# A planner's rule for work that two engines may do: GpSimd leaves it while VectorE has an earlier SBUF operation ready

## The chip, the core and the metric

The kernel runs on one core of a Trainium2 chip. The core has a matrix engine (TensorE, PE in the profile, with its weight loads as PEld), three elementwise engines (VectorE = DVE, ScalarE = ACT, GpSimd = POOL) and SyncE (SP), which here issues every DMA. Each engine runs its own list of instructions in order and waits on semaphores for the others. SBUF is the memory that all engines read; PSUM is where TensorE writes. The metric is the device time of one execution in microseconds, as the median of several runs.

## The reference

One inference step of a two-layer network on two groups of tokens with shared weights, 512 latent and 128 context tokens, 640 in all, width 1024:

```
for each of 2 layers:
  shift, scale, gate (twice) from SiLU(cond) @ ada_w + ada_b
  h = x * (1 + scale) + shift;  one projection h @ w_in, split among
    A  retention, both directions       B  gated linear attention, both directions
    C  differential attention (two softmax maps)      and three sigmoid merge gates
  merged = sum of sigmoid(m) * (y @ w_branch);  x = LayerNorm(ALPHA*x + gate * merged @ w_out)
  h = x * (1 + scale) + shift;  a, b = h @ ffn_w_up
  x = LayerNorm(ALPHA*x + gate * (gelu(conv3(a)) * b) @ ffn_w_down)
```

It returns both groups' outputs, and the context tokens' attention keys and values and final states.

## The kernel before

Activations stay in SBUF, features on the 128 partitions and the 640 tokens along a row: 8 rows of 128x640 are one activation. Weights are streamed in blocks of 128x1024 (`weights`, two blocks ahead of use, three buffers each for `w`, `whi` and `wlo`). Every product of float32 numbers is made of three fast ones: each operand is split into a rounded part and the rest (`whi` = rounded `w` on ScalarE, `wlo = w - whi`), and `gemm` adds hi\*hi, hi\*lo and lo\*hi. Tokens are handled in two halves, 384 and 256 wide, at the ends of a block of layers, so that a norm's first half runs beside the products of the second.

The kernel doesn't issue instructions directly. The text adds operations to a `Program` in the order in which the algorithm is written down; each has its possible engines, a cost per engine, its operands, and a key: its place in the text, plus `late` (the norm's operations have -300, so they count as 300 places earlier). `Program.order` calls `place`, a list scheduler: it keeps for every engine the time from which it is free and two heaps, `now` (operations ready by then, by key) and `later` (by the time from which they could start), picks a candidate for every engine, and places the candidate that starts first (a tie goes to the engine that stands first in PE, ACT, DVE, POOL, SP). The result, a list in order of planned start, is what the chip is given; the chip's engines then wait for what they need.

Most operations have one engine. Those marked `ANY` may go to VectorE or GpSimd, and these are the shared work of the title: `wlo` of every weight block, the rests `sal`, `vl`, `sql` of activations (`parts`), `ql` (`twice`), `kk` and `qd` (`stack`), and the chained sums of squares `sq` in `norm`. Planned costs in ns of n elements a row: 150 + 1.042 n on VectorE, 150 + 2.2 n on GpSimd. GpSimd also has work of its own: sums of gates `g`, rotary `sw`, decays `G`, `H`, `la`, and the rescaling of `xa`.

The plan has a `port`: a time before which no operation of that engine may start if its list `port` names the engine. An operation with SBUF operands alone names both ("DVE" and "POOL"); one that reads PSUM names only "POOL", so a VectorE operation that reads PSUM neither waits for the port nor takes it. Choosing for GpSimd, `place` looks first through `now`; a shared operation there is left waiting if VectorE would finish it no later. Candidates taken from `later` are not asked that. VectorE is asked before GpSimd, and its candidate has then been taken off `now["DVE"]`.

The norms, at four places, are these: a product with a matrix of 1/1024 gives the mean in PSUM (`pm`), VectorE subtracts it from eight rows `xa` (in the second half from a copy `mu` in SBUF), ScalarE squares, sums of squares give the variance, Ln and Exp on ScalarE give `rs`, and `hf`, `hh`, `hl` are the next products' operands. VectorE adds the products' results to `xa` before that (`xa<-pout` and `xa<-pdn`, the residual).

Of the kernel before, what the change touches and what calls it, by code (L numbers as in the profile page):

```python
# [223 lines left out]
class Program:  # L224
# [69 lines left out]
    def place(self, ahead, ahead_load, fences):  # L294
        import heapq
        engs = ("PE", "ACT", "DVE", "POOL", "SP")
        free = {e: 0.0 for e in engs}
        now, later = {e: [] for e in engs}, {e: [] for e in engs}
# [17 lines left out]
        def slots(op, t0):  # L316

            used = {}
            for t in op.tiles:
                if t.slot is None and t.pool is not None:  # L320
                    p = t.pool
                    u = used.get(p, 0)
                    used[p] = u + 1
                    if len(p.free) <= u + sum(n for (q, f), n in fences.items() if q is p and not f.eng and op.idx > f.idx):
                        p.blocked.append(op)
                        return None
                    if p.inorder or len(p.free) <= p.reserve:
                        while p.want[p.ptr][1].slot is not None:
                            p.ptr += 1
                        i, rank = p.ptr, 0  # L330
                        lim = 1 if p.inorder else len(p.free)
                        while rank < lim and p.want[i][1] is not t:
                            rank += p.want[i][1].slot is None
                            i += 1
                        if rank >= lim:
                            p.blocked.append(op)
                            return None
                    t0 = max(t0, heapq.nsmallest(u + 1, p.free)[u][0])
            return t0
# [4 lines left out]
        while len(done) < len(self.ops):  # L344
            best = None
            for e in engs:
                f, n, q = free[e], now[e], later[e]
                while q and (q[0][0] <= f or q[0][2].eng):
                    r, i, op = heapq.heappop(q)
                    if not op.eng:  # L350
                        heapq.heappush(n, (i, op))
                cand, skipped, waiting = None, [], []
                while n or q:
                    if n:
                        i, op = heapq.heappop(n)
                        if op.eng:
                            continue
                        t = slots(op, f)
                        if t is not None and e in op.port:
                            t = max(t, port)  # L360
                        if t is None:
                            op.queues.discard(e)
                            continue
                        if t > f:
                            heapq.heappush(q, (t, i, op))
                            continue
                        if e == "POOL" and len(op.engs) > 1 and max(free["DVE"], op.ready) + op.cost["DVE"] <= t + op.cost[e]:
                            waiting.append((i, op))
                            continue
                        if e == "ACT" and op.func in TABLES and not table & TABLES[op.func] and passed < 6 and len(skipped) < 6 \  # L370
                                and op.key[0] >= op.idx:
                            skipped.append((i, op))
                            continue
                        cand = (t, i, op)
                        break
                    if skipped:
                        break
                    r, i, op = heapq.heappop(q)
                    if op.eng:
                        continue  # L380
                    t = slots(op, r)
                    if t is not None and e in op.port:
                        t = max(t, port)
                    if t is None:
                        op.queues.discard(e)
                        continue
                    if t > r:
                        heapq.heappush(q, (t, i, op))
                        continue
                    cand = (t, i, op)  # L390
                    break
                if cand is None and skipped:
                    i, op = skipped.pop(0)
                    cand = (f, i, op)
                for x in skipped + waiting:
                    heapq.heappush(n, x)
                if cand is not None:
                    if best is None or cand[0] < best[0][0]:
                        if best is not None:
                            heapq.heappush(later[best[1]], best[0])  # L400
                        best = (cand, e)
                    else:
                        heapq.heappush(later[e], cand)
# [1351 lines left out]
```

## Time and profile before

| | |
|---|---|
| median of 3 runs | 2501.42 us (2501.3 to 2507.76) |
| the profiled execution | 2504.05 us, span 2502.3 us, granted clock 0.995 |
| TensorE busy | 2441.7 us (98% of the span) |
| VectorE, ScalarE, GpSimd busy | 1618.1, 1113.7, 528.8 us |
| wlo on VectorE | 268 instructions, 340.8 us, 1273 ns each |
| wlo on GpSimd | 50 instructions, 123.7 us, 2477 ns each |

The first part of the page gives busy time and its share of the span for each engine; a busy TensorE may still be slower than its best, since its products overlap. The line "A <- B: t, n, m" of the waits says that A waited for B for t us in total, n times, at most m. A line of the timeline gives start, duration, engine, source line and operation; "x2" means that two like instructions in a row were merged.

### The profile page before, as it was taken

What the parts mean: (1) busy time and instruction counts of PE and PEld (TensorE: products, weight loads), DVE (VectorE), ACT (ScalarE), POOL (GpSimd) and SP (SyncE); (2) the same over time, 40 slices, a digit from 0 to 9 for tenths busy, and PEclk for the clock granted to TensorE, in tenths of its full rate; (3) what the DMA queues carried; (4) which work ended last, traced back from release to release, by engine and by line L of the source; (5) the groups of instructions that cost most, each with busy time, mean ns of one, the idle gap of its engine ahead of it and who ended that gap; (6) DMA issues with size and microseconds to landing.
All of it is one profiled execution on the core that took longest, in us unless ns stands there. A gap on an engine that the chain in (4) does not pass through costs nothing.

```text
span 2502.3 us, 41620 instructions
## 1 busy us (share of the span) xinstructions
PE 2441.7 (98%) x16826; PEld 2328.8 (93%) x16826; DVE 1618.1 (65%) x2902; ACT 1113.7 (45%) x1815; POOL 528.8 (21%) x389
## 2 busy tenths in 40 slices
PE   8999999999999999999989999999999999999997
PEld 4898999999998999999978999999999999999997
DVE  4677778667798955656867677675454764343446
ACT  3576655444426322213456676554444353132234
POOL 0433112002153500000346521111013341000001
PEclk9999999999999999999999999999999999999999
DMA  7213222342543333333432133222314222222222
GB/s 291 79 60 123 100 87 89 113 161 86 185 136 103 126 109 118 104 125 124 137 101 84 64 127 101 87 95 70 107 67 144 94 84 76 76 73 71 77 77 87
DMA packets 99551, 263.85 MB, mean 105 GB/s; under 512 B 11168, under 2 KB 17696, under 8 KB 99232
## 3 DMA queue, kind: packets, MB, share of 16 engines
q1 hardware_dynamic: 99360, 261.21, 31.1%
q8 instruction: 132, 2.16, 0.4%
q14 instruction: 59, 0.48, 0.1%
HBM read 243.34 MB, written 17.83 MB: 104 GB/s over the span
## 4 chain that ended last, share of the span: by engine, by line
PE 90%; DVE 6%; ACT 2%; issue 1%; DMA 1%; SPq 0%; ACTq 0%; DVEq 0%
PE pmm L536 12%; PE pfb L536 12%; PE pfa L536 12%; PE pdn L536 12%; PE pvv L536 7%; PE pbr L536 6%; PE pout L536 4%; PE pcq L536 2%; PE pck L536 2%; PE pag L536 2%; PE psc L545 2%; PE pr L536 2%; PE ptc L536 1%; PE psl L545 1%; PE paq L536 1%
## 5 line engine op out<-in xcount | busy, mean ns | idle before, releaser
L557 ACT ACTIVATE whi<-w 128x1024 fp32r<-128x1024 f32 (+1 forms) x318 | 330.6, 1041 | 813.6 <-PE pdn L536 218.7
L569 DVE TENSOR_TENSOR wlo<-w,whi 128x1024 fp32r<-128x1024 f32 (+1 forms) x268 | 340.8, 1273 | 328.6 <-ACT whi L557 324.7
L569 POOL TENSOR_TENSOR wlo<-w,whi 128x1024 fp32r<-128x1024 f32 (+2 forms) x50 | 123.7, 2477 | 1190.9 <-ACT whi L557 991.5
L536 PE MATMUL pmm<-hh,whi 128*128 128x384 f32 (+1 forms) x768 | 240.9, 314 | 0.0
L536 PE MATMUL pmm<-hh,wlo 128*128 128x384 f32 (+1 forms) x768 | 240.7, 313 | 0.0
L536 PE MATMUL pmm<-hl,whi 128*128 128x384 f32 (+1 forms) x768 | 240.2, 313 | 0.0
L536 PE MATMUL pfa<-hh,whi 128*128 128x384 f32 (+1 forms) x704 | 218.1, 311 | 2.4 <-ACT hh L557 2.3
L536 PE MATMUL pfa<-hl,whi 128*128 128x384 f32 (+1 forms) x704 | 217.4, 310 | 2.6 <-DVE hl L583 2.6
L536 PE MATMUL pdn<-fl,whi 128*128 128x384 f32 (+1 forms) x704 | 218.5, 310 | 0.0
L536 PE MATMUL pdn<-fh,whi 128*128 128x384 f32 (+1 forms) x704 | 218.1, 310 | 0.0
L536 PE MATMUL pfb<-hh,whi 128*128 128x384 f32 (+1 forms) x704 | 217.9, 310 | 0.0
L536 PE MATMUL pfb<-hh,wlo 128*128 128x256 f32 (+1 forms) x704 | 217.4, 309 | 0.4 <-DVE wlo L569 0.4
L536 PE MATMUL pdn<-fh,wlo 128*128 128x384 f32 (+1 forms) x704 | 217.8, 309 | 0.0
L536 PE MATMUL pfa<-hh,wlo 128*128 128x384 f32 (+1 forms) x704 | 217.7, 309 | 0.0
L536 PE MATMUL pfb<-hl,whi 128*128 128x384 f32 (+1 forms) x704 | 217.4, 309 | 0.0
L536 PEld LDWEIGHTS pmm<-hh,whi 128*128 128x128 f32 x768 | 144.6, 188 | 3.1 <-issue 0.5
L536 PEld LDWEIGHTS pmm<-hh,wlo 128*128 128x128 f32 x768 | 144.6, 188 | 3.0 <-issue 1.1
L536 PEld LDWEIGHTS pmm<-hl,whi 128*128 128x128 f32 x768 | 144.5, 188 | 1.7 <-issue 0.5
L536 PE MATMUL pvv<-whi,hh 128*128 128x256 f32 (+1 forms) x480 | 137.4, 287 | 2.0 <-ACT whi L557 1.1
L536 PE MATMUL pvv<-wlo,hh 128*128 128x256 f32 (+1 forms) x480 | 136.0, 285 | 1.4 <-ACT z L557 0.7
L536 PE MATMUL pvv<-whi,hl 128*128 128x256 f32 (+1 forms) x480 | 136.7, 285 | 0.5 <-ACT z L557 0.4
L536 PEld LDWEIGHTS pfa<-hh,whi 128*128 128x128 f32 x704 | 132.6, 189 | 4.0 <-ACT hh L557 4.0
(395 smaller groups left out, 6797.0 us busy)
## 6 DMA issues: line engine op xcount, KB each, us to landing
w<-W SPq DMA_DIRECT2D x270, 512.0 KB, 3.5
wada<-adaT SPq DMA_DIRECT2D x160, 256.0 KB, 3.9
w<-W SPq DMA_DIRECT2D x42, 448.0 KB, 3.2
gate<-g SPq DMA_DIRECT2D x32, 320.0 KB, 2.3
g<-gate SPq DMA_DIRECT2D x32, 320.0 KB, 4.7
wada<-adaW SPq DMA_DIRECT2D x32, 256.0 KB, 6.2
x<-xT SPq DMA_DIRECT2D x8, 320.0 KB, 6.4
dist<-rc SPq DMA_DIRECT2D x8, 320.0 KB, 4.3
```

The lines of the kernel that those rows point to most:

```text
L536: prog.add(("PE",), lambda e: nc.tensor.matmul(real(out), real(lhsT), real(rhs), start=start, stop=stop), [out], [lhsT, rhs], {"PE": c})
L545: nc.tensor.matmul(real(o), real(w), real(r), start=start, stop=stop)
L557: prog.add(("ACT",), lambda e: nc.scalar.activation(out=real(out), in_=real(in_), func=func, **{k: real(x) for k, x in kw.items()}), [out] ...
L569: prog.add(eng, lambda e: ENG[e].tensor_tensor(out=real(out), in0=real(a), in1=real(b), op=op), [out], [a, b], vcost(out.n), late=late, po ...
```

## The change

One condition is added to the choice for GpSimd. A shared operation in GpSimd's `now` is left waiting as before if VectorE would finish it no later, and now also if VectorE's `now` holds another operation, not yet placed, whose port names "DVE" (its operands are in SBUF) and whose key is lower.

```
--- before.py
+++ after.py
@@ -364,7 +364,9 @@
                         if t > f:
                             heapq.heappush(q, (t, i, op))
                             continue
-                        if e == "POOL" and len(op.engs) > 1 and max(free["DVE"], op.ready) + op.cost["DVE"] <= t + op.cost[e]:
+                        if e == "POOL" and len(op.engs) > 1 and (
+                                max(free["DVE"], op.ready) + op.cost["DVE"] <= t + op.cost[e]
+                                or any(x is not op and not x.eng and "DVE" in x.port and x.key < op.key for _, x in now["DVE"])):
                             waiting.append((i, op))
                             continue
```

What is left waiting stays in both engines' heaps and is looked at again in the next round; GpSimd goes on to the next operation. No operation, operand, cost or buffer is changed; the list of instructions that comes out can differ in which of the two engines does a shared operation and in the order of everything planned after it.

## The prediction

> **What bounds the kernel now.** I read the page's first part, then the busy time by stage, then what TensorE waited for in the stages where it idles, then the groups and the order of time of VectorE (DVE) and GpSimd (POOL) there. The first part settles most of it:
>
> ```profile
> span 2502.3 us, 41620 instructions
> PE 2441.7 (98%) x16826; PEld 2328.8 (93%) x16826; DVE 1618.1 (65%) x2902; ACT 1113.7 (45%) x1815; POOL 528.8 (21%) x389
> ```
>
> TensorE idles for 2502.3 - 2441.7 = 60.6 us. No product is added or removed, so 60.6 us is all that a better order could give back, and only where it idles because of the elementwise engines. The stretches, cut where the work changes:
>
> ```profile
> 0.00:50.00 50.00, 39.86 (x235) 20.92 (x236) 21.18 (x78) 15.82 (x34) 2.86 (x9) 0.90 0.93 346
> 50.00:700.00 650.00, 640.69 (x4552) 601.48 (x4552) 472.86 (x867) 360.06 (x643) 150.77 (x120) 1.00 0.32 108
> 700.00:812.00 112.00, 104.12 (x670) 99.37 (x669) 99.39 (x193) 49.46 (x77) 49.98 (x24) 1.00 0.35 118
> 812.00:1205.00 393.00, 393.00 (x2683) 393.00 (x2682) 262.94 (x527) 106.73 (x122) 49.78 (x33) 1.00 0.35 116
> 1205.00:1345.00 140.00, 129.61 (x889) 120.65 (x889) 110.23 (x184) 73.38 (x126) 72.10 (x58) 0.99 0.36 115
> 1345.00:1930.00 585.00, 579.91 (x4086) 544.50 (x4083) 369.73 (x603) 319.38 (x566) 128.04 (x101) 1.00 0.28 95
> 1930.00:2050.00 120.00, 116.90 (x763) 113.80 (x762) 83.05 (x145) 54.57 (x83) 46.04 (x22) 0.99 0.28 93
> 2050.00:2430.00 380.00, 380.00 (x2594) 380.00 (x2594) 152.43 (x221) 101.32 (x114) 21.39 (x22) 1.00 0.23 75
> 2430.00:2503.00 73.00, 57.63 (x371) 55.09 (x369) 46.33 (x90) 33.00 (x54) 7.80 (x5) 0.92 0.27 87
> ```
>
> The columns are the length, then busy PE, PEld, DVE, ACT, POOL, the granted clock, the DMA share and GB/s. TensorE idles 10.1 us in the start, 9.3 in the mixers of layer 0, 7.9 at its first norm, nothing in its feed-forward part, 10.4 at its second norm, 5.1 in the mixers of layer 1, 3.1 at its first norm, nothing in its feed-forward part, and 14.7 (to the span's end) at the last norm and store. In the two feed-forward parts, 773 us, VectorE or GpSimd can be late without any price until a product waits. What counts is the four norms. There TensorE waited, in the windows from 760, 1248, 1995 and 2460 us:
>
> ```profile
> PE pfa L536 <- ACT hh L557: 1.5, 2, 0.8
> PE pfa L536 <- DVE hl L583: 1.3, 1, 1.3
> PE pm L536 <- DVE xa L583: 0.8, 1, 0.8
> ```
> ```profile
> PE pq L536 <- DVE hl L583: 2.7, 2, 2.1
> PE pm L536 <- DVE xa L583: 1.6, 1, 1.6
> ...
> PE pq L536 <- ACT hh L557: 0.2, 1, 0.2
> ```
> ```profile
> PE pfa L536 <- DVE hl L583: 1.3, 1, 1.3
> PE pm L536 <- DVE xa L583: 0.9, 1, 0.9
> PE pfa L536 <- ACT hh L557: 0.8, 1, 0.8
> ```
> ```profile
> PE pm L536 <- DVE xa L583: 1.3, 2, 0.7
> ```
>
> For the residual xa 0.8 + 1.6 + 0.9 + 1.3 = 4.6 us; for the next input, hl and hh, 1.3 + 2.7 + 1.3 + 1.5 + 0.2 + 0.8 = 7.8. Together 12.4 us hang on VectorE and its chain at the norms.
>
> **Part 1: which choices the new test reaches.** It is asked where the old one was: in the branch for an operation that was ready when GpSimd finished its last one, with the planner's port free at that moment. An operation that becomes ready while GpSimd idles, or that the port pushed back, comes from the other heap (`later`), where nothing is asked. Two more limits: VectorE's own candidate was taken off `now["DVE"]` before GpSimd's turn, so there must be a second earlier ready operation; and a VectorE operation that reads PSUM has no "DVE" in its port and doesn't count. Of the 96 shared instructions on GpSimd in the trace, I count 24 that start within 0.2 us of the end of GpSimd's instruction before (six of them wlo). The first and the last, each with the row that starts its run, and the clearest pair of wlo:
>
> ```profile
> 223.38 1.29 POOL L569 TENSOR_TENSOR kk<-ek,kk 64x512 fp32r<-64x512 f32 x1 [7.03 <-DVE wlo L569]
> 224.74 1.83 POOL L569 TENSOR_TENSOR ql<-eq,qq 64x512 fp32r<-64x512 f32 x1
> ...
> 2463.35 2.15 POOL L569 TENSOR_TENSOR wlo<-w,whi 128x896 fp32r<-128x896 f32 x1 [391.75 <-ACT whi L557]
> 2465.46 3.23 POOL L569 TENSOR_TENSOR sq<-sq 128x384 f32<-128x384 f32 x3
> ```
> ```profile
> 768.31 6.88 POOL L569 TENSOR_TENSOR wlo<-w,whi 128x1024 fp32r<-128x1024 f32 x2 [3.08 <-ACT whi L557]
> ```
>
> The old test already refuses a wlo unless VectorE is taken for 2403 - 1217 = 1186 ns more (the planner's costs for 1024 elements). So the new one bites between two PSUM operations in a row, or on short operations. The chained squares have a key 300 places early, so hardly anything stands ahead of them. I take half of the 24 as refused: three wlo, nine short ones. Ends: none, and all 24.
>
> **Part 2: what a refused wlo costs and frees.**
>
> ```profile
> L569 POOL TENSOR_TENSOR wlo<-w,whi 128x1024 fp32r<-128x1024 f32 x37 | 94.5, 2560 | 575.2 <-ACT whi L557 561.0 <-PE pmm L536 10.6 <-PE pm L536 3.4
> ...
> L569 DVE TENSOR_TENSOR wlo<-w,whi 128x1024 fp32r<-128x1024 f32 x233 | 302.1, 1298 | 309.4 <-ACT whi L557 306.0
> ```
>
> Three moved wlo take 3 x 2.56 = 7.7 us from GpSimd and put 3 x 1.30 = 3.9 us on VectorE. Behind a wlo on VectorE stand the residual sums; behind the buffers of w, whi and wlo (three each, in order) stand ScalarE's next whi and SP's next weight load, with the ada loads after it in the queue; the matrix product of that block waits for it. The nearest row for that wait is the one for wlo on VectorE now, the only three such waits of the whole run:
>
> ```profile
> PE pvv L536 <- DVE wlo L569: 0.7, 1, 0.7
> ...
> PE pfb L536 <- DVE wlo L569: 0.4, 1, 0.4
> PE pk L536 <- DVE wlo L569: 0.4, 1, 0.4
> ```
>
> So a moved wlo costs TensorE between 0 and its 1.3 us; I take 0.5, near those rows: 3 x 0.5 = +1.5 us. Its cover is the two blocks of weights held ahead; without it each costs its full 1.3.
>
> What is freed is the port. In order of time VectorE, while GpSimd ran the pair from 768.31 to 775.19:
>
> ```profile
> 770.31 0.88 DVE L583 SCALAR_TENSOR_TENSOR xa<-pout,gh,xa 128x256 f32<-128x256 f32 x2
> 771.11 4.70 DVE L569 TENSOR_TENSOR xa<-xa,mu 128x256 f32<-128x256 f32 x3
> 775.73 0.47 DVE L583 SCALAR_TENSOR_TENSOR xa<-pout,gh,xa 128x256 f32<-128x256 f32 x1
> ```
> ```profile
> L569 DVE TENSOR_TENSOR xa<-xa,mu x32: 409/415/2605, 769.6 to 2483.3; 128x256 f32<-128x256 f32 x32
> ```
>
> Three subtractions took 4.70 us where the shortest takes 409 ns (least, median and longest stand in the second row); the residual at 775.73 came after them, and the product pm waited 0.8 us for it. The operation that reads PSUM was not stretched: 0.47 us. The Trainium skill, "SBUF — State Buffer", "Who interferes with whom", calls this an exclusive lock: a VectorE instruction with two SBUF inputs fully blocks against a GpSimd one that reads SBUF. The trace agrees with the 2605 ns beside 409; taken alone the rule speaks for the change, and its result is the faster rival below.
>
> Were the second wlo of the pair refused (the trace doesn't show by which branch it was chosen), the subtractions would run first. I count the residual's wait as gone at the two first norms (0.8 and 0.9 us, the layers repeat each other): -1.7 us. The chain after it (mean, variance, Ln, Exp, hf, hh, hl) then has ScalarE late next, so hl and hh I leave at 0; ends: 0 and the whole -12.4.
>
> **Part 3: the short operations** (ql, kk, qd, sq). In the mixers they lie beside 97 to 99% of TensorE; I cost nine of them at 0, cover being that TensorE has other products. Without the cover each could cost as much as it takes on GpSimd now, 1.83 us for the ql above, so 9 x 1.83 = 16.5 us is the far end upward; downward the mixers' idle 9.3 + 5.1 = 14.4 us. Neither end is near: the waits there are many and under 1 us.
>
> **Sum.** +1.5 - 1.7 + 0 = -0.2 us. The profiled execution took 2504.05 us (span 2502.3 and 1.75 around it), so 2503.9 for its like; it stands 2.6 us above the median of 2501.42 (2501.3 to 2507.76), so the median should be 2501.2.
>
> **The rivals.** A: the plan does not change, because no choice meets all the conditions of part 1. For it: the branch `later` and the old test. Against: 24 candidates, and one differing choice is enough. Time 2501.4.
>
> B, faster: each norm's pairs are separated, VectorE clears its subtractions early, and the whole chain moves. For it: the 4.70 us and 12.4 us of waits. Against: most wlo at the norms start after a gap on GpSimd, so nothing asks; and the start and the tail's store stay. All of it gives 2501.4 - 12.4 = 2489.0; from 7.5 us on, 60% of it, it decides.
>
> C, slower: at the two first norms a refused wlo keeps queueing on VectorE, which is 99.39 of 112 us busy at the first. I count seven wlo on GpSimd there from 756 to 784 us and seven in the same place of layer 1. All on VectorE: 14 x 1.30 = 18.2 us; with half of it hidden, 9.1 on the path: 2510.5. It decides from six unhidden wlo on (7.8 us). For it: products of the second half are short there, so weights are wanted fast. Against: only three such waits exist now, and GpSimd's long hold goes with each.
>
> **How the numbers follow.** About 0.3%, 7.5 us, is what a measurement here can tell from no change. Likeliest case (few choices, near nothing) 0.58 and A 0.14; B 0.13; C 0.15. The first two lie within 0.3% but for a small part either way that I give to the reshuffling of later picks, which B and C as often fall short of: same 0.73, faster 0.13, slower 0.14. The range reaches toward B and C until about one in ten is left out on each side: 2493 to 2510 us.
>
> **What would show it.** TensorE busy stays at 2442 us within 3. GpSimd's wlo fall from 50 to 44 to 49 and its shared instructions from 96 to some 84; VectorE's wlo rise by as many. The pair at 768 us is split and the three subtractions near 0.4 us each; pm's wait for xa at the two first norms goes below 0.5 us. In the feed-forward parts TensorE still idles for nothing. Wrong would be: new waits of the products for wlo of over 1 us each (C), the waits for hl and hh gone together (B), or a different order of products in the mixers with idle time there well off 9.3 and 5.1 us.

## The result: 0.6% slower, nearly all of it in the attention of the two layers

The changed kernel took 2521.02 us (median of 6 runs, 2517.89 to 2523.1); the kernel before, run beside it, 2505.36 us (6 runs, 2501.3 to 2511.76). The ratio is 1.0064 [1.0052, 1.0076], some 15.7 us. (Over all 63 executions of the kernel before that are on record the median is 2506.86, 14.2 us below.) The two profiled executions differ by as much: span 2518.1 us against 2502.3. The first part of the page after:

```profile
span 2518.1 us, 41604 instructions
PE 2447.7 (97%) x16826; PEld 2332.7 (93%) x16826; DVE 1614.8 (64%) x2893; ACT 1115.6 (44%) x1818; POOL 538.9 (21%) x395
```

The same products are in the list (16826), yet TensorE is busy for 6.0 us more and idles for 70.4 us instead of 60.6: 9.8 us more. GpSimd, which a stricter rule should have relieved, does more: 538.9 us for 528.8, and counted through its groups, 102 shared instructions for 96, of which 53 wlo for 50.

Where the time is, by stretch, in the columns and cuts of the prediction (the later stretches lie up to 16 us earlier in the work than they do before):

```profile
50.00:700.00 650.00, 635.87 (x4505) 595.28 (x4506) 465.19 (x850) 358.11 (x639) 152.88 (x123) 1.00 0.32 107
...
1345.00:1930.00 585.00, 575.94 (x4056) 538.70 (x4055) 365.93 (x599) 319.22 (x569) 133.85 (x107) 1.00 0.28 94
```

In the two feed-forward parts TensorE still idles for almost nothing (0.4 us of 393 and 0.0 of 380). The mixers of layer 0 lose 4.8 us of TensorE (640.69 to 635.87), those of layer 1 4.0 (579.91 to 575.94). A sharper cut is by products: a stage runs from the first product of one tile to the first of the next. A row of one tile gives the least, median and longest duration in ns, then the first start of all and the last. Before, then after, the first query product of the differential attention (`pcq`) and the first product of w_out (`pout`), layer 0:

```profile
L536 PE MATMUL pcq<-hh,whi x128: 276/334/448, 379.7 to 1798.7; 128*128 128x384 f32 x64, 128*128 128x256 f32 x64
L536 PE MATMUL pout<-mh,whi x256: 274/333/573, 713.9 to 2006.8; 128*128 128x384 f32 x64, 128*128 128x256 f32 x64
```
```profile
L538 PE MATMUL pcq<-hh,whi x128: 275/332/448, 377.7 to 1814.8; 128*128 128x384 f32 x64, 128*128 128x256 f32 x64
L538 PE MATMUL pout<-mh,whi x256: 274/332/575, 719.1 to 2022.8; 128*128 128x384 f32 x64, 128*128 128x256 f32 x64
```

From `pcq` to `pout` layer 0 took 713.9 - 379.7 = 334.2 us before and 719.1 - 377.7 = 341.4 after. Below, this stage is called the attention. Cut so from TensorE's order of time (first `paq` product for the start, `pfa` for the end of the norm), in us:

| profiled execution | start | attention, layer 0 | first norm, layer 0 | attention, layer 1 | first norm, layer 1 |
|---|---|---|---|---|---|
| before | 245.65 | 334.26 | 69.81 | 333.24 | 65.57 |
| after | 243.71 | 341.40 | 73.65 | 340.14 | 65.47 |
| difference | -1.9 | +7.1 | +3.8 | +6.9 | -0.1 |

The other stages agree within about 1 us. The +14.0 of the two attentions is the change. The +3.8 and -1.9 aren't: the planned order there is the same in both kernels, and kernels of the experiments with that same order spread over 69.75 to 73.78 us at the norm (before, e2 and e4; after, e5, e6 and e7), and the starts of after, e5, e6 and e7 over 243.71 to 246.81.

In the attention of layer 0 TensorE's gaps grew from 3.6 to 8.4 us, and its busy time from 330.6 to 333.0; in layer 1 from 2.9 to 6.9, and from 330.3 to 333.3. In layer 1 up to 1.7 us of that is a stretch at half the granted clock (0.50 from 1719.8 to 1723.2 us; none in either attention before); the other growth of the busy time I didn't take apart. TensorE's waits in the whole run, those with new or grown entries:

```profile
PE pm L538 <- DVE xa L585: 6.8, 5, 3.0
...
PE ptc L538 <- ACT at L559: 3.6, 5, 1.2
...
PE pvv L538 <- ACT whi L559: 3.0, 4, 0.9
...
PE pvv L538 <- POOL wlo L571: 2.8, 2, 1.5
```

The first is the norm's (4.6 us before). The other three stand in the attention, but for 1.1 us of `pvv`'s waits for whi, which stand behind the second norm as they did before: before, in the attention `ptc` waited for no `at`, `pvv` for no whi, and no product for a wlo of GpSimd.

**What the new test did.** Followed through the planner's choices, it refused three operations in the whole program, all of them rests of cached keys. None is a wlo, and only two came later by it: in each layer one rest of a cached key, `kk<-ck`, 64x128, about 0.8 us of work at the start of the attention. GpSimd's order of time there in layer 0, before and then after:

```profile
391.19 2.19 POOL L569 TENSOR_TENSOR kk<-ck,kk 64x128 fp32r<-64x128 f32 x2
394.96 1.29 POOL L569 TENSOR_TENSOR ql<-qc,qq 64x512 fp32r<-64x512 f32 x1 [1.58 <-ACT qq L557]
```
```profile
389.23 1.32 POOL L571 TENSOR_TENSOR kk<-ck,kk 64x128 fp32r<-64x128 f32 x1
393.01 1.29 POOL L571 TENSOR_TENSOR ql<-qc,qq 64x512 fp32r<-64x512 f32 x1 [2.46 <-ACT qq L559]
395.44 1.70 POOL L571 TENSOR_TENSOR sw<-sw,cst 128x512 f32<-128x512 f32 x1 [1.13 <-DVE sw L603]
397.22 0.81 POOL L571 TENSOR_TENSOR kk<-ck,kk 64x128 fp32r<-64x128 f32 x1
```

The second rest went from the end of a pair to 7.99 us behind the first, after `ql` and `sw`. No product waited for it. But every choice that the planner makes after that point stands on other times, and the lists differ from there to the end of the attention.

**What the new lists have in them.** A score tile `psc` takes both PSUM buffers of its pool and is made of four pairs of products, added as four operations. TensorE after, the tile that starts at 443.30:

```profile
443.30 0.46 PE L547 MATMUL psc<-kk,qq 128*128 128x320 f32 x2
443.68 0.41 PE L547 MATMUL psc<-kk,ql 64*128 64x320 f32 x2
...
461.74 0.46 PE L547 MATMUL psc<-kk,qq 128*128 128x320 f32 x2
462.13 0.41 PE L547 MATMUL psc<-kk,ql 64*128 64x320 f32 x2
```

The tile belongs to head 1, started early; its second half stands late in the text, and the gate products `pmm` pass it for 18 us. Both buffers are held meanwhile, so the last `ptc` of head 0 has none, and the planner's window for loads, counted from the first product not yet placed, stands still. SP's queue before, and then after, with the weight loads `w<-W`:

```profile
443.93 0.39 SPq L621 DMA_DIRECT2D w<-W  x1
...
446.89 2.69 SPq L621 DMA_DIRECT2D w<-W  x2
```
```profile
443.15 19.84 SPq L623 DMA_DIRECT2D gate<-g  x3
...
463.56 0.91 SPq L623 DMA_DIRECT2D w<-W  x2
```

The busy times there, before and after:

```profile
440.00:462.00 22.00, 22.00 (x154) 21.97 (x154) 18.94 (x40) 14.29 (x21) 0.93 (x1) 1.00 0.64 228
462.00:476.00 14.00, 14.00 (x107) 13.17 (x105) 9.36 (x20) 4.38 (x7) 0.00 (x0) 1.00 0.31 100
```
```profile
440.00:462.00 22.00, 22.00 (x150) 21.58 (x148) 4.03 (x8) 4.95 (x9) 2.84 (x1) 1.00 0.08 31
462.00:476.00 14.00, 10.16 (x70) 8.84 (x69) 8.14 (x13) 9.18 (x16) 2.58 (x2) 1.00 0.79 295
```

While the half tile stands, VectorE is busy for 4.03 of 22 us instead of 18.94, ScalarE for 4.95 instead of 14.29, and the DMA share is 0.08 instead of 0.64. TensorE doesn't notice: it has the gates' products. The price comes right after: 3.84 us without a product between 462 and 476, on `at`, wlo and whi. From 440 to 500 TensorE's waits of over 0.2 us were these after:

```profile
PE ptc L538 <- ACT at L559: 2.2, 3, 1.2
PE pvv L538 <- POOL wlo L571: 1.4, 1, 1.4
PE pvv L538 <- ACT whi L559: 0.9, 1, 0.9
```

and before only 0.4 us, once, for `qkp`.

### The profile page after: what moved, and what is told of

It reads as the page before. It is cut to its first block, busy times and chain, and to the rows that moved or that the text cites. A ratio compares the mean times of both kernels' runs of the same rounds, so it can differ in the third digit from the quotient of the medians.

```text
span 2518.1 us, 41604 instructions
## 1 busy us (share of the span) xinstructions
PE 2447.7 (97%) x16826; PEld 2332.7 (93%) x16826; DVE 1614.8 (64%) x2893; ACT 1115.6 (44%) x1818; POOL 538.9 (21%) x395
## 4 chain that ended last, share of the span: by engine, by line
PE 88%; DVE 6%; ACT 2%; issue 1%; DMA 1%; POOL 0%; SPq 0%; ACTq 0%; DVEq 0%; POOLq 0%
PE pmm L538 12%; PE pfb L538 12%; PE pfa L538 12%; PE pdn L538 12%; PE pvv L538 7%; PE pbr L538 5%; PE pout L538 3%; PE pcq L538 2%; PE pck L538 2%; PE pag L538 2%; PE pr L538 2%; PE psc L547 2%; PE ptc L538 1%; PE psl L547 1%; PE paq L538 1%
## 5 line engine op out<-in xcount | busy, mean ns | idle before, releaser
L559 ACT ACTIVATE whi<-w 128x1024 fp32r<-128x1024 f32 (+1 forms) x318 | 330.3, 1041 | 802.4 <-PE pdn L538 220.0
L571 POOL TENSOR_TENSOR wlo<-w,whi 128x1024 fp32r<-128x1024 f32 (+2 forms) x53 | 130.5, 2465 | 1179.4 <-ACT whi L559 978.8
```

The source lines that it names most:

```text
L559: prog.add(("ACT",), lambda e: nc.scalar.activation(out=real(out), in_=real(in_), func=func, **{k: real(x) for k, x in kw.items()}), [out] ...
L571: prog.add(eng, lambda e: ENG[e].tensor_tensor(out=real(out), in0=real(a), in1=real(b), op=op), [out], [a, b], vcost(out.n), late=late, po ...
```

## The experiments

Theory P: the loss is made in the plan, by the half-started tile. Rivals: the late rest itself; the amount of work on GpSimd; the position of a single operation in a list, which then could be put back by hand.

**One operation for a score tile** (`e1_one_op_scores`), on the changed kernel:

```
+    def mm_all(*ms):
+        ...  # one "PE" operation that issues all products of ms
     ...
+    ms = []
     for hf in range(2):
         ...
-        mm_pair(*((out[m], qq[m][:, c], kk[m][:, d]) for m in range(2)), stop=False)
-        mm_pair(*((out[m], ql[a, c], kk[m][a, d]) for m, a in enumerate(rows)), start=False)
+        ms += [(out[m], qq[m][:, c], kk[m][:, d], True, False) for m in range(2)]
+        ms += [(out[m], ql[a, c], kk[m][a, d], False, True) for m, a in enumerate(rows)]
+    mm_all(*ms)
```

> The changed kernel, with the eight products of one score tile of mixer C (both halves of the keys, both maps) entered in the planner as one operation, so that a half-started tile can't hold the pair of PSUM buffers; the rule and its refusals stay. Theory P (the refused 64x128 rest only re-deals the picks around it; what costs is that a score tile starts half, keeps both PSUM buffers for 18 us, and the planner's window for loads stands still meanwhile): the time falls back to that of before, 2501 to 2507 us, and psc's halves stand next to each other. Rival S (the share of VectorE and GpSimd is what costs: more GpSimd work holding the port): the rests on GpSimd still differ from before, so it stays above 2515 us.

Measured: 2505.85 us against 2507.31, ratio 0.9989 [0.9979, 0.9999]; attentions 334.47 and 333.39 us. The tile that was torn apart, in TensorE's order of time of this kernel, and all that TensorE waited for from 440 to 500:

```profile
444.89 0.46 PE L555 MATMUL psc<-kk,qq 128*128 128x320 f32 x2
445.28 0.41 PE L555 MATMUL psc<-kk,ql 64*128 64x320 f32 x2
445.63 0.56 PE L555 MATMUL psc<-kk,qq 128*128 128x320 f32 x2
446.12 0.41 PE L555 MATMUL psc<-kk,ql 64*128 64x320 f32 x2
```
```profile
PE pcq L538 <- ACT qkp L568: 0.4, 1, 0.4
```

Two of the refusals and both late rests are still there, the order still isn't that of before, GpSimd still has 51 wlo; the loss is gone. With the tile as one operation the changed kernel is as fast as the kernel before. No run has the one operation without the new test; the planner, run on that text, gives a plan that ends when this one does (below).

**The late rest alone** (`e2_rest_moved_alone`): the list of the kernel before, with the two rests placed 7.71 us later in it, the distance in the changed plan, and nothing planned anew.

```
 ops = prog.order(ahead=AHEAD, ahead_load=AHEAD_LOAD)
+for o in ops:
+    if o.idx in (4380, 14886):     # kk<-ck of layer 0, of layer 1
+        o.start += 7710
+ops.sort(key=lambda o: (o.start, o.idx))
 ...
```

> The plan of the kernel before; in it only the one refused rest kk<-ck of each layer starts 7.71 us later in the plan (behind a ql and a sw on GpSimd), nothing is planned anew. Theory P: the late rest itself costs nothing, 2501 to 2507 us. Rival L (the refused operation is late for the one that waits for it, the cost that the prediction named): 5 us or more above the kernel before.

Measured: 2508.28 against 2507.31, ratio 1.0002 [0.9993, 1.0012], attentions 334.26 and 333.24 us, to 0.01 us those of before. The median lies 1.3 us over the range stated; that of the kernel before beside it lies 0.3 over it too. What was moved costs nothing; so the cost lies in what was planned after it.

**One layer at a time** (`e3_first_layer_only`, `e4_second_layer_only`): the new test with one more term.

```
-or any(x is not op and ... and x.key < op.key for _, x in now["DVE"])):
+or any(x is not op and ... and x.key < op.key for _, x in now["DVE"]) and op.idx < 9000):   # e4: > 9000
```

> The new test counts only for operations of layer 0. Theory P: mixer C of layer 0 shows its 7 us and the first norm perhaps its 3.8 us, mixers of layer 1 as before: 2509 to 2513 us. Rival N (the difference is spread or comes from the chip's own variation): no such split between the two layers.

> The new test counts only for operations of layer 1. Theory P: only mixer C of layer 1 is longer, by 6.8 us, and the first norm is as before: 2508 to 2511 us. Rival N: no such split between the two layers.

Measured: 2511.26, 1.0019 [1.0009, 1.0029], and 2512.43, 1.0021 [1.0011, 1.0030], both against 2507.31. The attentions took 342.92 and 333.32 us in the first, 334.26 and 339.74 in the second: each layer pays for its own refusal. By stages the two add up to 8.7 + 6.5 = 15.2 us, beside 14.0 in the changed kernel; e3's first attention has the changed kernel's order and is 1.5 us longer, with a stretch at half the granted clock (475.5 to 478.9 us) that the changed kernel's profile doesn't have there. By the medians the two add up to 4.0 + 5.1 = 9.1 us of 15.7, and e4's lies 1.4 us over its range. The first norm's spread, below, could hide the rest; that wasn't shown and stays open.

**Putting single things back** (`e5_tile_finished_at_once`, `e6_loads_ahead_of_store`, `e7_both_moves`): the changed kernel's list, with only the tile's second half moved right behind its first on TensorE (e5), only three weight loads per layer moved ahead of the gate's store on SP (e6), or both (e7).

```
+# e5, e7: for every psc tile whose third and fourth pair start over 5 us after its first
+o.start = first[0] + 300 * (first[1] - 1)
+# e6, e7: for the three loads of w behind the store of gate{l}23, sp[i]
+o.start = sp[i].start - 40 + 10 * k
```

> The plan of the changed kernel; in it only the second half of the score tile that stood 18 us behind its first half is put right behind it on TensorE, in both layers; the other engines' lists stay. Theory P: VectorE and ScalarE get that tile early and the products ptc no longer wait for at, some 2 us less for each layer; the loads are still late: 2514 to 2518 us. Rival D (the late loads are all of the cost): no change, 2519 to 2523 us.

> The plan of the changed kernel; in it only three weight loads of each layer are put ahead of the last store of a gate on SyncE's queue (gate023 and gate123), behind which they stood. Theory P: the waits of pvv for whi and wlo go (2.3 us in layer 0, 2.4 in layer 1), the rest stays: 2515 to 2518 us. Rival D (the late loads are all of the cost): 2505 to 2509 us.

> Both moves of the two kernels beside it in the plan of the changed kernel. Theory P: they add up, 4 us for each layer: 2511 to 2515 us; the rest of the 14 us stays, since what was planned after them is still planned around the held buffers. Rival D: as with the loads alone, 2505 to 2509 us.

Measured, against 2505.38: 2520.44, 1.0061 [1.0043, 1.0079]; 2519.89, 1.0055 [1.0038, 1.0072]; 2522.1, 1.0068 [1.0053, 1.0083]. None gained, so I was wrong on all three. Rival D (the late loads are all of the cost) said so of e5 alone, and fell with e6 and e7; none of the positions put back by hand gave any of the time back. ScalarE's order of time in e5 shows why:

```profile
463.29 0.70 ACT L559 ACTIVATE g<-pmm 128x640 f32<-128x640 f32 x1 [9.79 <-PE pmm L538]
463.89 0.79 ACT L559 ACTIVATE pc<-psc,mx 128x640 f32<-128x640 f32 x1
```

VectorE had the tile's maximum by 448, but ScalarE's list still had the sigmoid of a gate ahead of the Exp `pc`, and stood 9.79 us for that gate's product. In e6 the loads went early on SP's queue and ScalarE converted them as late as in the changed kernel (there at 472.22, with a start 3.1 us earlier), behind `at`, `oc` and the squares:

```profile
455.73 1.39 SPq L623 DMA_DIRECT2D w<-W  x3
```
```profile
475.36 2.94 ACT L559 ACTIVATE whi<-w 128x1024 fp32r<-128x1024 f32 x3
```

Every engine's list was written round the late half tile. Taking it away by hand in one or two lists leaves the third; planning anew without it (e1) takes it out of all.

**The test asked in every branch** (`e8_test_asked_always`): also of candidates from `later`.

```
+if e == "POOL" and len(op.engs) > 1 and any(x is not op and not x.eng and "DVE" in x.port and x.key < op.key for _, x in now["DVE"]):
+    waiting.append((i, op))
+    continue
 cand = (t, i, op)
```

> The new test is asked also of shared operations taken from the other heap (later), which is how most of GpSimd's shared work is chosen. Theory P: what decides is how mixer C comes out after the first differing pick, not how much work moves: some 2510 to 2520 us, with about 22 fewer shared instructions on GpSimd than before. Rival S (what costs is shared work on GpSimd holding the port): clearly faster than before, below 2498 us.

Measured: 2517.21 against 2505.38, 1.0048 [1.0033, 1.0063]. GpSimd now has 74 shared instructions and is busy for 474.3 us, and the kernel is still slower than before, though the two first norms are 1.5 and 2.7 us shorter (68.27, 62.91 us). The attentions are as before (333.93, 332.42 us), and the loss sits in another place, the second norm of layer 0 and the products behind it: from the first `pdn` product to the next layer's first `pcq` 726.0 us, before 712.9. TensorE's waits there, and the end of that stretch:

```profile
PE pq L541 <- ACT hh L562: 10.7, 1, 10.7
PE pq L541 <- DVE wlo L574: 7.6, 1, 7.6
```
```profile
1270.00:1290.00 20.00, 9.57 (x45) 8.98 (x46) 16.54 (x22) 4.25 (x9) 18.34 (x16) 0.60 0.21 61
```

The granted clock of 0.60 is that of a stretch at half clock, from 1265.7 to 1286.2 us, in which TensorE was busy for 5.75 us. The time fell in the range that theory P gave, but not where it looked for it, in the attention: in that the number is luck. In the narrow form "the half tile is the one thing that can go wrong" the theory doesn't cover this. The broad form does: a new rule moves the plan to another order, and what that order costs isn't in the moved operations.

**The norm's pair on VectorE** (`e9_norm_pair_on_vectore`): the kernel before; at each layer's first norm the two wlo that GpSimd runs among the eight subtractions of the mean go to VectorE, behind the fifth and the eighth.

```
+for g in (mu[0:8], mu[16:24]):      # the subtractions xa<-xa,mu of the two first norms
+    pair = [...]                    # GpSimd's two wlo between g[0] and g[7]
+    for o, x in zip(pair, (g[4], g[7])):
+        o.eng, o.start = "DVE", x.start + 1
```

> The plan of the kernel before; in it, at the first norm of each layer, the two wlo that GpSimd does among the eight subtractions xa<-xa,mu go to VectorE, one behind the fifth subtraction, one behind the eighth. This is the move that the prediction took for likely there. Theory R (GpSimd's pair and the subtractions race for the shared reads, and who comes first by a few tenths of a us makes 69.8 or 73.8 us of the stretch from the first pout to the first pfa): the subtractions take about 0.4 us each, the products' wait for xa is under 0.5 us, the stretch of layer 0 is 68 to 70 us, time 2499 to 2505 us. Rival W (the weights' rests then come late, the prediction's case C): new waits for wlo of about 1 us, no gain or a loss.

Measured: 2500.91 against 2506.85, 0.9979 [0.9967, 0.9991]: about 6 us faster than the kernel before, the fastest of all. VectorE's order of time at the first norm of layer 0:

```profile
773.90 1.09 DVE L569 TENSOR_TENSOR xa<-xa,mu 128x256 f32<-128x256 f32 x3
774.90 3.42 DVE L569 TENSOR_TENSOR wlo<-w,whi 128x1024 fp32r<-128x1024 f32 x1
```

Three subtractions in 1.09 us where the prediction's row had 4.70; the three before them, at 769.78, took 1.09 us too. One wlo of VectorE is now the one that is held up (3.42 us). `pm` no longer waits for `xa` at either first norm; these norms took 68.93 and 64.61 us in the profile, 0.9 and 1.0 less than before. That is 1.8 us in one pair of profiles against 6 in the medians; the difference would fit the two lengths of this norm in the last section, since without the pair there is no race to lose. The spread points the same way: seven executions within 3.7 us, the nineteen of the kernel before within 10.4. One profile can't show it.

**Keeping heads apart** (`e10_heads_kept_apart`), on the changed kernel: the first score tile of a head may be planned only after the fourth tile's last product of the head before.

```
-mm_pair(*((out[m], qq[m][:, c], kk[m][:, d]) for m in range(2)), stop=False)
+mm_pair(*((out[m], qq[m][:, c], kk[m][:, d]) for m in range(2)), stop=False,
+        after=last[0] if t == 0 and hf == 0 else None)
```

> The changed kernel; in it the first score tile of each next head of mixer C waits for the fourth tile's last product of the head before, so a later head can't take the PSUM buffers from an earlier one. Theory P (the overtaking after the refusal is what costs): mixer C comes out near 334 us in layer 0 instead of 341 for the most part; with what the plan still re-deals 2505 to 2511 us. Rival Q (the overtaking is only one of many ways in which the re-dealt plan is worse): 2515 to 2523 us, as the changed kernel.

Measured: 2510.95 against 2506.85, 1.0018 [1.0008, 1.0029]. The attention of layer 1 is back at 334.13 us, 0.9 over before. That of layer 0 is at 339.53, with 2.2 us of waits between 440 and 500 in which a score tile `psc` waits for `pc` on ScalarE, waits that neither other kernel has. So in layer 1 the loss goes when the next head may not overtake; in layer 0 forbidding it gives a third order with a loss of its own, which I didn't take apart.

**The plan's own times.** The loss can be read without the chip: `order` gives every operation a planned start and end. Worked out by running the planner in the text of each kernel that plans anew, the end of the last operation, beside the medians (each against the kernel before of its own session):

| kernel | plan ends, us | against before, planned | against before, measured |
|---|---|---|---|
| before | 2449.7 | | |
| after | 2465.1 | +15.4 | +15.7 |
| e1 | 2449.7 | 0.0 | -1.5 |
| e3 | 2459.2 | +9.5 | +4.0 |
| e4 | 2455.6 | +5.9 | +5.1 |
| e8 | 2462.1 | +12.4 | +11.8 |
| e10 | 2455.7 | +6.0 | +4.1 |

The plan of before with the score tile as one operation and without the new test also ends at 2449.7. In the plan of after the +15.4 is +9.5 and +5.9 in the two attentions and nothing elsewhere; in that of e8 it is +10.1 between `pdn` and the next `pcq`. So the loss stood in the plan, in the planner's own costs, before anything ran. What the medians differ from it by, 5.5 us at most (e3), may lie in the first norm, whose length varies by 4 us with one list (last section); no run pins it there.

## Why the prediction was wrong

**What held.** TensorE is the bound, and its feed-forward parts hide everything. The limits read out of part 1, above all that candidates from `later` aren't asked, are why so little was refused: in the plan of before only seven shared operations come to the point where the new test decides, in that of after eight. Rival C's cause, wlo on VectorE waited for by products, didn't come: no wlo was refused. Rival A's premise nearly held too: three refusals, two of them of any effect. The price that part 2 put on the norms' pair, 1.7 us at the two first norms, was borne out by e9's profile, 1.8 us; only the change doesn't touch that pair.

**Part 1, the count.** "Half of the 24, three wlo, nine short ones" was a middle between ends. It was three, all of them short. The step before it failed: a start within 0.2 us of the end of GpSimd's last instruction, 24 times in the trace, was taken for a choice that the test reaches; in the plan only seven operations reach it. Of the eight in the plan of after, three found an earlier operation in VectorE's heap.

**Part 3, the step that failed.** "The short operations lie beside 97 to 99% of TensorE; I cost nine of them at 0", with the reshuffling of later picks as "a small part either way". e2 shows the first half right, for the two that came later, to 0.01 us an attention. The second half was the whole result: +7.1 and +6.9 us from two operations of 0.8 us. My upper end, nine times the operation's own length, was reckoned along the path of the moved operation; that its 16.5 us lies near the 15.7 measured is chance, since two operations made the loss and not by their length. The cost came along another path: a different pick some 50 us later starts a tile that takes all of a pool and doesn't finish it. That the plan can do this stood in the text of the kernel: `psc` takes two buffers at once, its four pairs are four operations with their own keys, and the planner may place others between them. No row of before shows it, because before's plan happened not to do it; this was an unpriced risk with ends on both sides, and needed a case of its own. It could have had a number: the changed plan's own end, 15.4 us later, is in the text of the kernel and asks for no run.

**The forecasts of the last part.** TensorE busy rose by 6.0 us, not within 3. Some of it is the half clock: after the start there are three more stretches of 3.4 us at half clock than before, one of them behind the norm's longer wait (last section), and one fewer in the start. The rest I didn't take apart. GpSimd's wlo rose to 53 and didn't fall; its shared instructions rose to 102. The pair at the first norm stayed:

```profile
773.74 5.84 POOL L571 TENSOR_TENSOR wlo<-w,whi 128x1024 fp32r<-128x1024 f32 x2 [3.41 <-ACT whi L559]
```
```profile
774.74 5.13 DVE L571 TENSOR_TENSOR xa<-xa,mu 128x256 f32<-128x256 f32 x2
```

and `pm`'s wait there grew from 0.8 to 2.97 us. (That is no effect of the new test: the planned order there is the one of before.) The one sign named for a wrong forecast that did come is "a different order of products in the mixers with idle time there well off 9.3 and 5.1 us": it is now 14.1 and 9.1.

## What to carry to other kernels

Where a list scheduler writes the order, a change of rule isn't priced by the operations that it moves but by the plan that comes out from the first differing choice on; follow that plan and read its own end time (here 15.4 us planned, 15.7 measured), or allow for a loss or gain many times the moved work. Work that holds a scarce buffer until its last part is done should be one operation for the scheduler: that made this kernel insensitive to the same rule (e1). And when such a plan has gone wrong, moving one operation back in one engine's list gains nothing while the other lists are still written round it.

## What was unexpected of the hardware

**Two lengths of one norm from one list.** The first norm of layer 0 took 69.81 us before and 73.78 in e4, where the list there is the same; in the changed kernel, again with that list, 73.65, and 69.75 in e5. (The 72.06 us of e3, with that list too, are the slow form without the half clock of the next paragraph.) In the slow form two subtractions of 0.41 us take 5.13 us, and GpSimd's first wlo 3.4 to 3.7; in the fast form two get through in 0.75 us, GpSimd's first wlo takes 4.4, and the next subtractions are caught. In both GpSimd's wlo starts ahead of the subtractions. The fast form, before, VectorE from a wlo of its own on, and GpSimd's first wlo:

```profile
768.03 1.21 DVE L569 TENSOR_TENSOR wlo<-w,whi 128x1024 fp32r<-128x1024 f32 x1
...
769.64 0.75 DVE L569 TENSOR_TENSOR xa<-xa,mu 128x256 f32<-128x256 f32 x2
```
```profile
768.31 4.37 POOL L569 TENSOR_TENSOR wlo<-w,whi 128x1024 fp32r<-128x1024 f32 x1 [3.08 <-ACT whi L557]
```

The slow form, e4, likewise:

```profile
765.04 1.21 DVE L571 TENSOR_TENSOR wlo<-w,whi 128x1024 fp32r<-128x1024 f32 x1
...
766.64 5.12 DVE L571 TENSOR_TENSOR xa<-xa,mu 128x256 f32<-128x256 f32 x2
```
```profile
765.28 3.72 POOL L571 TENSOR_TENSOR wlo<-w,whi 128x1024 fp32r<-128x1024 f32 x1 [3.06 <-ACT whi L559]
```

GpSimd's wlo starts 0.28 us behind VectorE's in the fast form and 0.24 in the slow one, so the order of starts that the profile shows doesn't tell who is held up; what decides stays open. The Trainium skill, "SBUF — State Buffer", "Who interferes with whom", says that issue order and not the shape of the operations decides who blocks. The trace agrees that the shape doesn't: the same two kinds of operation, at 0.75 us the two or 5.13 us the two. Of the issue order it shows no more than these starts.

**The granted clock after a wait of 2 to 3 us.** In the changed kernel, the 3.41 us in which most of the 2.97 us wait at the first norm lies, and the next:

```profile
777.74:781.15 3.41, 0.75 (x3) 0.67 (x4) 3.41 (x5) 0.84 (x3) 1.84 (x1) 1.00 0.61 178
781.15:784.57 3.42, 3.42 (x13) 2.79 (x12) 0.50 (x2) 1.74 (x2) 0.00 (x0) 0.50 0.75 283
```

and in e3, with a wait of 2.98 us in the same place:

```profile
779.33:782.74 3.41, 1.76 (x8) 1.42 (x9) 2.90 (x6) 1.85 (x3) 0.83 (x1) 1.00 0.67 244
782.74:786.15 3.41, 3.41 (x26) 3.24 (x26) 1.49 (x4) 3.22 (x5) 1.37 (x1) 1.00 0.48 185
```

The clock (third column from the right) falls to half for 3.41 us in the first and not at all in the second, and the norm took 73.65 us in the first and 72.06 in the second. So a wait of 2 to 3 us can cost up to 1.7 us (half of 3.41) beyond itself, and it hangs on where it falls: in each of the twelve profiles the stretches at half clock start whole multiples of 3.41 us from one another. I counted these steps of 3.41 us over the twelve profiles, without the first 60 and the last 25 us. After a step at full clock the clock fell to half 46 times: after all 30 steps in which TensorE idled for over 1.8 us, after none with under 1.4 us, and after 16 of the 42 between. Above, 2.66 us of the step are idle in the changed kernel; in e3 the wait lies across two steps, and 1.65 us of the one shown are idle. The Trainium skill, "TensorE: Matmul & The Clock Gate", Part 1, gives an idle window of about 3.4 us ahead of the half clock; here the step has that length, and idling for about half of it was enough.
